# Hybrid pooling and state-space layer on one core: gate tiles reordered around the state-space projection, and branch merges cut into three steps

## The chip, the cores and the metric

The kernel runs on one core of a Trainium2 chip. The metric is device time in microseconds (us) of one launch. The engines are TensorE (PE, matrix products), VectorE (DVE), ScalarE (ACT), GpSimd (POOL, which here mostly issues transfers) and SyncE (SP, which issues the weight loads). Each engine takes its own instructions strictly in order and waits on semaphores for the others.

## What is computed

One layer of a hybrid encoder, in float32, for 256 prompt rows and 8 x 16 sample rows, so 384 rows (tokens) in all; model width 2048.

```python
proj  = rmsnorm(x) @ w_in                     # pool | z | xBC | dt | gates
gates = sigmoid(gate columns)                 # g_A and g_B, 2048 columns each
A     = pooled, mapped and scaled pool part   # 2048 wide
B     = gated_rmsnorm(ssd_scan(...), z)       # 4096 wide, norm over 8 groups of 512
m     = g_A * (A @ w_pool_proj) + g_B * (B @ w_ssd_proj)
x     = x + rmsnorm(m @ w_out)
x     = x + rmsnorm(relu(rmsnorm(x) @ w_up)**2 @ w_down)
```

The change lies around `B @ w_ssd_proj`, the product and sum that make `m`, and the start of `m @ w_out`.

## The kernel before, in words

**Products in float32.** Each float32 operand is split into a high part h and the rest l (fp32r). ACT makes h with a copy (L70 or L1120), DVE makes l with a subtraction (L71 or L1121). A product is three matmuls: h·h, l·h and h·l. Weights come in pieces of 128x1024 through SP.

**Gate tiles.** A gate tile is 128 of the 2048 gate columns for all 384 tokens. `proj` (L136) makes one in two halves; a half takes one weight piece and issues 24 matmuls (L101 to L103, 128x384). After each half a hook may run, which writes other work into the program at that point. `gate_b(i)` makes tile i of branch B: DVE scales it (L587), ACT takes the sigmoid (L588), POOL stores it in scratch memory `gb_scr` (L589). `gate_late(i)` makes tile i of branch A: scaling (L1311), sigmoid (L1312), then DVE multiplies it by the branch's pooled product, `ppt`, which POOL loads from `pp_scr` (L1309, L1313), and POOL stores the result in `ma_scr` (L1314). Gate work is issued on DVE and ACT behind the latest weight split (`later`).

**The last norm of branch B.** Before the stage begins, DVE normalises the last group of B (L191 to L193) and scales its four tiles (L925); POOL stores them in `a_scr` (L928). The projection reads B back from `a_scr` through SP (L1229, `ax`).

**The mixed stage.** `B @ w_ssd_proj` runs as 16 pairs ("quads") of seven forms each, 112 in all, which is Strassen's scheme with seven products for a two by two block. The weights of a form are b11, b21, U, b22, W, V or X; the activations are matching sums and differences. DVE makes the differences (L1235), ACT and DVE split them (L1242, L1243). U starts as the piece b12 in a buffer w_b, onto which POOL adds a second piece by an accumulating load (L1133). The forms are woven in between gate halves so that PE has both: the twelve tiles ga4 to ga15 (24 halves) and gb8 to gb12 (10 halves) call `hook`, 34 times in all. The first call takes the differences and four of the splits of quad 0, the second the other four, and from the third on `112 * (done - 2) // 32` forms have been issued. So three gate halves (ga4 and the first of ga5) stand on PE in front of the first form. Sums collect in `acc` (`acs`, `sq` in PSUM); at the end DVE turns each half of `acc` into four product blocks by seven additions (`converted`).

**The merges.** `merge(n)` makes tile n of m. POOL loads gate tile `gb` and the gated product `ma` (L1295, L1296), PE transposes three blocks of `acc` (L1299, tile `mt`), DVE multiplies (L1300) and adds (L1301), ACT and DVE split the result into mh and ml (L1302, L1303). Merges 0 to 3 lie inside the last quad, the tiles of the others, `gbr` and `mar`, have two buffers each.

**The last part.** Gate tiles gb13 to gb15 (six halves, no hook) follow, then the product with w_out: `moving` issues 18 matmuls (L154 to L156, 128x512) for a unit of 256 rows of w_out. Merges 4 and 5 stand ahead of unit 0, and merges 6+2i and 7+2i behind unit i, up to unit 4. The stage's memory is freed there, and units 5 to 7 come with the rest of w_out. Behind the layer's first half follow the up-projection (`pj_up`) and the down-projection, whose quads (`wd`) have the same seven forms and an accumulating load each.

Of the kernel before, what the change touches and what calls it, by code (L numbers as in the profile page):

```python
# [14 lines left out]
P = 128  # L15
T = 384
# [17 lines left out]
def build(ctx, tc, io):  # L34
    nc = tc.nc
    v, s, te, gp, sy = nc.vector, nc.scalar, nc.tensor, nc.gpsimd, nc.sync
# [179 lines left out]
    pp_scr = [dram.tile([P, T], F32, name=f"pp_scr{i}") for i in range(4, KD)]  # L216
# [871 lines left out]
    ms_ = []  # L1088
# [158 lines left out]
    def sp_quad(gk, np_):  # L1247
        def part(slot, k2):
            h, l = slots[gk][slot]
            return h[:, k2], l[:, k2]  # L1250

        def extra(i):
            t = np_ * 7 + i
            if gk and t < 3:
                refill(gk, ("W", "V", "X")[t])
            if gk == 7:
                if t in (7, 8):
                    for _ in range(4):
                        if todo:
                            todo.pop(0)()  # L1260
                elif 9 <= t < 13:
                    merge(t - 9)
                elif t == 13:
                    todo.extend(converted(lambda m: acc[:, 9 + m]))
                    while todo:
                        todo.pop(0)()
                elif t == 6:
                    todo.extend(converted(lambda m: acc[:, m]))
                elif t == 4:
                    spare.append(pq.tile([P, 10, 2, P], F32, tag="ax", name="axe").rearrange("p s k t -> p (s k t)"))  # L1270
# [12 lines left out]

    todo, spare = [], []

    def merge(n):
        if n < NE:
            gb, ma = (spare[0][:, i * T : i * T + T] for i in (n % 3 * 2, n % 3 * 2 + 1))
            h, l = early_tiles(("mh", "ml", ms_))
        else:  # L1290
            ma, gb = (mp.tile([P, T], F32, tag=f"{a}r", name=f"{a}r{n}", bufs=2) for a in ("ma", "gb"))
            h = mp.tile([P, T], F32R, name=f"mh{n}")
            l = mp.tile([P, T], F32R, name=f"ml{n}")
            ms_.append((h, l))
        gp.dma_start(gb, gb_scr[n])  # L1295
        gp.dma_start(ma, ma_scr[n])  # L1296
        o = sstile(f"mt{n}")[:, :T]
        for b in range(3):
            te.transpose(o[:, b * P : b * P + P], hacc(acc, b, n // 4)[:, n % 4 * P : n % 4 * P + P], ident)  # L1299
        v.tensor_tensor(gb, o, gb, ALU.mult)  # L1300
        v.tensor_tensor(ma, ma, gb, ALU.add)  # L1301
        s.activation(h, ma, AF.Copy)  # L1302
        v.tensor_tensor(l, ma, h.bitcast(F32), ALU.subtract)  # L1303

    def gate_late(i, hook):
        ps = proj([io["w_ga"][i, q] for q in range(2)], xg, f"ga{i}", hook)
        t = pq.tile([P, T], F32, tag="gt", name=f"gat{i}", bufs=2)
        pp = pq.tile([P, T], F32, tag="pt", name=f"ppt{i}")
        gp.dma_start(pp, pp_scr[i - 4])  # L1309
        with later():  # L1310
            v.tensor_tensor(halves(t), even_odd(ps), halves(rstd), ALU.mult)  # L1311
            s.activation(t, t, AF.Sigmoid)  # L1312
            v.tensor_tensor(t, t, pp, ALU.mult)  # L1313
        gp.dma_start(ma_scr[i], t)  # L1314

    aload(0)
    for gk in range(8):
# [3 lines left out]

    def hook():
        done_[0] += 1
        if done_[0] == 1:
            diffs(0)
            for key in ("b11", "s2", "b21", "U"):
                refill(0, key)
        elif done_[0] == 2:
            for key in ("b22", "W", "V", "X"):
                refill(0, key)  # L1330
        want = max(0, 112 * (done_[0] - 2) // (NH_ - 2))
        forms(want - done_[1])
        done_[1] = want

    for i in range(4, KD):
        gate_late(i, hook)
    for i in range(8, 13):
        gate_b(i, pq, "gt", hook, 2)
    assert not line
# [11 lines left out]
    def merges(*ns):  # L1351
        def go():
            for n in ns:
                merge(n)

        return go
# [39 lines left out]
    with tc.tile_pool(name="phf", bufs=1, side="right", reuse_waits="tile") as pf, tc.tile_pool(  # L1396
# [80 lines left out]
        for nb in range(4):  # L1477
            gpo = pf2.tile([P, 512], F32, tag="gpo", name=f"gpo{nb}", bufs=1)
            sy.dma_start(gpo, io["g_mix_post"][blk(nb)].partition_broadcast(P))
            s.activation(gpo, gpo, AF.Copy, scale=-0.5)  # L1480
            o = [sstile(f"wo{nb}_{b}") for b in range(3)] if nb else o_first

            def scaled(b, nb, o, gpo):
                return v.tensor_tensor(hm[:, b, blk(nb)], o[b], gpo, ALU.mult)

            def done(b):
                q = pf2.tile([P, 512], F32, tag="q", name=f"q1_{nb}_{b}", bufs=1)
                sq = lambda: s.activation(q, o[b], AF.Square, accum_out=st[:, b, nb : nb + 1])
# [18 lines left out]
            moving(  # L1507
                o,
                wo_units(nb),
                ms_,  # L1510
                5 if nb == 3 else 0,
                done,
                pk,
                5 if nb == 3 else 0,
                None,
                {(2, 3): first_turns} if nb == 3 else None,
                lo=0 if nb else 5,
            )
        phk.close()
        pga = upool.enter_context(tc.tile_pool(name="pga", bufs=1, reuse_waits="tile"))  # L1520
# [370 lines left out]
```

## Time and profile before

| | us |
|---|---|
| median of 3 runs | 2616.23 (2615.16 to 2618.46) |
| the profiled execution | 2614.65 |
| its span | 2612.7 |
| PE busy | 2580.1 |
| DVE busy | 1955.3 |
| ACT busy | 1597.7 |
| POOL busy | 425.4 |

The profile is of one execution. A span runs from the first to the last instruction; the profiled execution took 1.95 us more than its span. In a row of the timeline the columns are start, duration, engine, line, operation, what is written and what is read, and in brackets how long the engine had been idle and which instruction of which engine ended that. Rows with x2 or more are runs of equal instructions. A row of waits gives the sum, the count and the longest. A row of windows gives the stretch, its length and each engine's busy time (PE, PE's weight loads, DVE, ACT, POOL, with the number of instructions), then the clock that was granted to PE, the DMA engines' busy share and GB/s.

### The profile page before, as it was taken

To read this page: it belongs to the slowest core of one execution; us is meant where nothing else is said; L and a number is where in the kernel's file an instruction comes from. 1 tells how busy PE (TensorE), PEld (TensorE's weight loads), DVE (VectorE), ACT (ScalarE), POOL (GpSimd) and SP (SyncE) were. 2 spreads that over 40 slices of the span, in tenths; PEclk is the share of its full clock that TensorE was granted. 3 is DMA by queue.
4 is the path that set the end of the run, shared out by engine and by line. 5 is a ranking of instruction groups with operands and counts; after the bars stand their busy time and mean duration, and the time that the engine had idled before them with its cause. 6 is when DMAs were issued, how large, how long until landed. Compare 5 with 4: busy or idle time off the path is not lost.

```text
span 2612.7 us, 41084 instructions
## 1 busy us (share of the span) xinstructions
PE 2580.1 (99%) x15589; PEld 2452.8 (94%) x15589; DVE 1955.3 (75%) x2763; ACT 1597.7 (61%) x2520; POOL 425.4 (16%) x622
## 2 busy tenths in 40 slices
PE   9999999999999999899999989999999999999998
PEld 9999999999999999889999978999999999999997
DVE  6675367999999998588888755767777777777766
ACT  6443365657565756378888534666667676766653
POOL 0000043445444543110001010000000000000000
PEclk9999999999999999999999999999999999999999
DMA  7445466666666766576766365555545555555434
GB/s 277 150 137 163 158 223 212 238 214 234 228 238 209 237 228 226 198 220 196 209 192 204 132 214 172 198 161 167 154 151 157 167 171 154 154 153 163 143 133 174
DMA packets 151189, 490.42 MB, mean 188 GB/s; under 512 B 21728, under 2 KB 36896, under 8 KB 145232
## 3 DMA queue, kind: packets, MB, share of 16 engines
q1 hardware_dynamic: 111312, 358.29, 41.1%
q0 software_dynamic: 32624, 114.70, 15.4%
q10 hardware_dynamic: 7056, 14.81, 1.8%
q8 instruction: 122, 2.00, 0.3%
q14 instruction: 75, 0.61, 0.1%
HBM read 437.85 MB, written 49.87 MB: 187 GB/s over the span
## 4 chain that ended last, share of the span: by engine, by line
PE 95%; issue 2%; DVE 1%; DMA 1%; POOL 1%; ACT 0%; DVEq 0%; POOLq 0%; ACTq 0%
PE pj_up L101 6%; PE pj_up L103 6%; PE pj_up L102 6%; PE wd L1170 5%; PE wd L1169 5%; PE wd L1171 5%; PE pj_x L101 5%; PE pj_x L102 5%; PE pj_x L103 5%; PE pj_z L103 3%; PE pj_z L102 3%; PE pj_z L101 3%; PE sq L1170 3%; PE sq L1171 3%; PE sq L1169 3%
## 5 line engine op out<-in xcount | busy, mean ns | idle before, releaser
L101 PE MATMUL pj_up<-x1h,wh_up 128*128 128x384 f32 (+1 forms) x1024 | 333.7, 326 | 0.0
L102 PE MATMUL pj_up<-x1l,wh_up 128*128 128x384 f32 (+1 forms) x1024 | 333.4, 326 | 0.0
L103 PE MATMUL pj_up<-x1h,wl_up 128*128 128x384 f32 (+1 forms) x1024 | 333.4, 326 | 0.0
L70 ACT ACTIVATE wh_up<-w_up 128x1024 fp32r<-128x1024 f32 x126 | 133.2, 1057 | 219.6 <-PE pj_up L102 202.5
L101 PE MATMUL pj_x<-xgh,wh_x 128*128 128x384 f32 x768 | 251.9, 328 | 0.0
L102 PE MATMUL pj_x<-xgl,wh_x 128*128 128x384 f32 x768 | 250.4, 326 | 0.0
L103 PE MATMUL pj_x<-xgh,wl_x 128*128 128x384 f32 x768 | 250.4, 326 | 0.0
L71 DVE TENSOR_TENSOR wl_up<-w_up,wh_up 128x1024 fp32r<-128x1024 f32 x126 | 154.1, 1223 | 57.7 <-ACT wh_up L70 57.2
L102 PEld LDWEIGHTS pj_up<-x1l,wh_up 128*128 128x128 f32 x1024 | 193.6, 189 | 2.6
L101 PEld LDWEIGHTS pj_up<-x1h,wh_up 128*128 128x128 f32 x1024 | 193.6, 189 | 2.6
L103 PEld LDWEIGHTS pj_up<-x1h,wl_up 128*128 128x128 f32 x1024 | 193.6, 189 | 0.0
L101 PE MATMUL pj_z<-xgh,wh_z 128*128 128x384 f32 x512 | 166.9, 326 | 0.0
L102 PE MATMUL pj_z<-xgl,wh_z 128*128 128x384 f32 x512 | 166.9, 326 | 0.0
L103 PE MATMUL pj_z<-xgh,wl_z 128*128 128x384 f32 x512 | 166.9, 326 | 0.0
L1133 POOL DMA_DIRECT2D w_b_wd<-w_down x28 | 24.2, 865 | 773.2 <-DMA w_b_wd<-w_down 742.5
L101 PEld LDWEIGHTS pj_x<-xgh,wh_x 128*128 128x128 f32 x768 | 145.1, 189 | 2.1 <-issue 0.4
L102 PEld LDWEIGHTS pj_x<-xgl,wh_x 128*128 128x128 f32 x768 | 145.2, 189 | 0.0
L103 PEld LDWEIGHTS pj_x<-xgh,wl_x 128*128 128x128 f32 x768 | 145.2, 189 | 0.0
L71 DVE TENSOR_TENSOR wl_x<-w_x,wh_x 128x1024 fp32r<-128x1024 f32 x96 | 116.8, 1221 | 30.1 <-ACT wh_x L70 30.1
L70 ACT ACTIVATE wh_x<-w_x 128x1024 fp32r<-128x1024 f32 x96 | 100.3, 1052 | 59.9 <-PE pj_z L102 30.9
L1146 ACT COPY acc<-wd 128x512 f32<-128x512 f32 x200 | 116.5, 583 | 23.0 <-PE wd L1171 22.9
L1169 PE MATMUL wd<-wh_b_wd,fh 128*128 128x512 f32 x336 | 127.3, 379 | 0.0
(478 smaller groups left out, 7827.8 us busy)
## 6 DMA issues: line engine op xcount, KB each, us to landing
w_up<-w_up SPq DMA_DIRECT2D x128, 512.0 KB, 4.1
w_b_wd<-w_down SPq DMA_DIRECT2D x112, 512.0 KB, 4.5
w_x<-w_in SPq DMA_DIRECT2D x96, 512.0 KB, 4.0
w_z<-w_in SPq DMA_DIRECT2D x64, 512.0 KB, 4.0
w_b_sq<-w_ssd SPq DMA_DIRECT2D x64, 512.0 KB, 4.3
w_ga<-w_ga SPq DMA_DIRECT2D x32, 512.0 KB, 3.9
w_pp<-w_pp SPq DMA_DIRECT2D x32, 512.0 KB, 3.5
hs<-ssm POOLq DMA_DIRECT2D x16, 1024.0 KB, 7.2
```

The lines of the kernel that those rows point to most:

```text
L70: cut[0] = s.activation(h, w, AF.Copy)
L71: cut[1] = v.tensor_tensor(l, w, h.bitcast(F32), ALU.subtract)
L101: te.matmul(out, wh, xh, start=first, stop=False, **how)
L102: te.matmul(out, wh, xl, start=False, stop=False, **how)
L103: return te.matmul(out, wl, xh, start=False, stop=last, **how)
L1133: gp.dma_start(w, unit(0, np_ * 2), accum_op=ALU.add)
L1146: s.copy(dst, o)
L1169: te.matmul(out, mh, vh, start=begin, stop=False, skip_group_check=held)
L1170: te.matmul(out, mh, vl, start=False, stop=False, skip_group_check=held)
L1171: te.matmul(out, ml, vh, start=False, stop=end, skip_group_check=held)
```

## The change

Three things are moved.

- **First end.** gb8 and gb9 now come ahead of ga4, so four plain gate halves stand in front of the forms. Hooks 2 and 3 hold the differences and splits of quad 0, and the 112 forms are spread over 31 hooks in place of 32. In `gate_late` the product with `ppt` and the store in `ma_scr` are kept back (`late`) and issued at the first hook of the next gate tile, and the load of `ppt` is issued at the first hook of its own tile.
- **Merges.** `merge` becomes `fetch` (two loads), `gated` (transposes, multiply, add) and `parts` (the split). The tiles of merges 0 to 2 lie in the free `ax` buffer; the others, `mw`, in the seven buffers "wd" that held the quads' weights. A pair of loads now needs a buffer that was freed by the merge seven places before, in place of two.
- **Second end.** Inside the last quad DVE makes one addition of the first conversion for each form from t = 7 on, and no merge. The second conversion and merges 0 to 9 are put at the hooks of gb13 to gb15 (`turns`). During w_out block 0 the three steps of a merge stand behind different units; six units (not five) run before the stage's memory is freed.

```diff
@@ sp_quad.extra, last quad
-                if t in (7, 8):
-                    for _ in range(4):
-                        if todo:
-                            todo.pop(0)()
-                elif 9 <= t < 13:
-                    merge(t - 9)
-                elif t == 13:
-                    todo.extend(converted(lambda m: acc[:, 9 + m]))
-                    while todo:
-                        todo.pop(0)()
+                if t == 4:
+                    early = pq.tile([P, 10, 2, P], F32, tag="ax", name="axe").rearrange("p s k t -> p (s k t)")
+                    for n in range(3):
+                        place[n] = early[:, n * 768 : n * 768 + 768]
+                        fetch(n)
                 elif t == 6:
                     todo.extend(converted(lambda m: acc[:, m]))
+                elif t > 6:
+                    todo.pop(0)()
@@ gate_late
+        def both():
+            if not pp:
+                while late:
+                    late.pop(0)()
+                pp.append(pq.tile([P, T], F32, tag="pt", name=f"ppt{i}"))
+                gp.dma_start(pp[0], pp_scr[i - 4])
+            hook()
...
-            v.tensor_tensor(t, t, pp, ALU.mult)
-        gp.dma_start(ma_scr[i], t)
+        def product():
+            v.tensor_tensor(t, t, pp[0], ALU.mult)
+            gp.dma_start(ma_scr[i], t)
+        late.append(product)
@@ hook and the gate tiles
-        want = max(0, 112 * (done_[0] - 2) // (NH_ - 2))
+        want = max(0, 112 * (done_[0] - 3) // (NH_ - 3))
...
+    for i in range(8, 10):
+        gate_b(i, pq, "gt", hook, 2)
     for i in range(4, KD):
         gate_late(i, hook)
-    for i in range(8, 13):
-        gate_b(i, pq, "gt", hook, 2)
+    for i in range(10, 13):
+        gate_b(i, pq, "gt", hooked, 2)
...
+    turns = [
+        do((gated, (0, 1)), (parts, (0, 1))),
+        do((gated, (2,)), (parts, (2,)), (fetch, (6, 7))),
+        do((gated, (3, 4)), (parts, (3,))),
+        do((close_half, (0,)), (gated, (5, 6))),
+        do((fetch, range(8, 11)), (gated, (7, 8))),
+        do((gated, (9,))),
+    ]
+    do((fetch, (3, 4, 5)))()
     for i in range(13, KD):
-        gate_b(i, pq, "gt", None, 2)
+        gate_b(i, pq, "gt", lambda: turns.pop(0)(), 2)
...
-    merge(4)
-    merge(5)
-    moving(o_first, wo_units(0), ms_, 0, None, None, 0, {i: merges(6 + 2 * i, 7 + 2 * i) for i in range(5)}, lo=0, hi=5)
+    do((parts, (4, 5)), (fetch, (11, 12)))()
+    between_ = {
+        0: do((parts, (6, 7)), (fetch, (13, 14)), (gated, (10,))),
+        1: do((parts, (8, 9)), (fetch, (15,)), (gated, (11,))),
+        2: do((parts, (10, 11)), (gated, (12,))),
+        3: do((parts, (12,)), (gated, (13,))),
+        4: do((parts, (13,)), (gated, (14, 15))),
+        5: do((parts, (14, 15))),
+    }
+    moving(o_first, wo_units(0), ms_, 0, None, None, 0, between_, lo=0, hi=6)
```

How the change moves instructions is seen in three places. The first is DVE at the first end, from the last of the four products on the last group of B. Before (`gat` is gate tile ga4, `alb` and `als` the low parts of the activations, `ax` the differences of quad 0):

```order
L925 SCALAR_TENSOR_TENSOR zs_3_11577<-zs_3_11577,vec,ny_g_12299 128x384
L1311 TENSOR_TENSOR gat_12436<-pj_ga_12338,rstd 128x384
L1313 TENSOR_TENSOR gat_12436<-gat_12436,ppt_12437 128x384
L1243 TENSOR_TENSOR alb_12375<-ax_12333,ahb_12374 128x256
L1243 TENSOR_TENSOR als_12379<-ax_12333,ahs_12378 128x256
L1235 TENSOR_TENSOR ax_12333<-ax_12333 128x256 x5
```

The same place now, with `gbt` for the gate tiles gb8 and gb9:

```order
L925 SCALAR_TENSOR_TENSOR zs_3_11577<-zs_3_11577,vec,ny_g_12299 128x384
L587 TENSOR_TENSOR gbt_12420<-pj_gb_12338,rstd 128x384
L1243 TENSOR_TENSOR alb_12405<-ax_12333,ahb_12404 128x256
L1243 TENSOR_TENSOR als_12409<-ax_12333,ahs_12408 128x256
L587 TENSOR_TENSOR gbt_12563<-pj_gb_12424,rstd 128x384
L1235 TENSOR_TENSOR ax_12333<-ax_12333 128x256 x5
```

The product that reads `ppt` no longer stands ahead of the differences; the scaling of gb9 stands there, which reads the PSUM tile of the fourth gate half and writes a tile whose memory held the last of the four products (`zs_3`), so that it also waits until POOL's store of that tile has landed.

The second place is POOL's queue in the mixed stage, at the accumulating load of the fifth quad (`w_b_sq_0`). Before:

```order
L1314 DMA ma_scr_123<-gat_13069 128x384
L1309 DMA ppt_13294<-pp_scr_108 128x384
L1133 DMA w_b_sq_0_13331<-w_ssd 128x1024
L1314 DMA ma_scr_124<-gat_13293 128x384
L1309 DMA ppt_13510<-pp_scr_109 128x384
```

And now:

```order
L1327 DMA ma_scr_121<-gat_13012 128x384
L1316 DMA ppt_13048<-pp_scr_106 128x384
L1133 DMA w_b_sq_0_13357<-w_ssd 128x1024
L1327 DMA ma_scr_122<-gat_13229 128x384
L1316 DMA ppt_13265<-pp_scr_107 128x384
```

The load stands behind the gated product of ga5 (121) where it stood behind that of ga7 (123).

The third place is POOL's queue at the second end, from the store of gate tile gb13 (`gb_scr_145`) on. Before, from there to the fourth pair of loads:

```order
L589 DMA gb_scr_145<-gbt_16028 128x384
L589 DMA gb_scr_146<-gbt_16093 128x384
L1295 DMA gbr_16171<-gb_scr_136 128x384
L1296 DMA mar_16170<-ma_scr_120 128x384
L589 DMA gb_scr_147<-gbt_16158 128x384
L1295 DMA gbr_16185<-gb_scr_137 128x384
L1296 DMA mar_16184<-ma_scr_121 128x384
L1295 DMA gbr_16223<-gb_scr_138 128x384
L1296 DMA mar_16222<-ma_scr_122 128x384
```

And now, from the same store:

```order
L589 DMA gb_scr_145<-gbt_16024 128x384
L1284 DMA mw_16165<-gb_scr_142 128x384
L1285 DMA mw_16165<-ma_scr_126 128x384
L589 DMA gb_scr_146<-gbt_16124 128x384
L589 DMA gb_scr_147<-gbt_16216 128x384
L1284 DMA mw_16236<-gb_scr_143 128x384
L1285 DMA mw_16236<-ma_scr_127 128x384
L1284 DMA mw_16239<-gb_scr_144 128x384
L1285 DMA mw_16239<-ma_scr_128 128x384
```

At the store of gb14 the loads stood at merge 4 (`gb_scr_136`) and now stand past merge 10 (`gb_scr_142`); the last loads, of merges 13 to 15 (`gb_scr_145` to 147), still follow the stores of the gate tiles that they read.

More of the change, by code (lines that the diff above doesn't have):

```diff
@@ L1282, in sp_quad, with fetch, gated @@
         return quad(f"sq{gk}_{np_}", pq, acc, np_, gk == 0, lambda i, nb: io["w_ssd"][nb, gk * 2 + i], part, extra)
[L1284 to L1296, printed above, removed]
+    todo, place = [], {}
+    def fetch(n):
+        if n not in place:
+            place[n] = pq.tile([P, 1024], F32, tag="wd", name=f"mw{n}", bufs=7)
+        gp.dma_start(place[n][:, :T], gb_scr[n])
+        gp.dma_start(place[n][:, T : 2 * T], ma_scr[n])
+    def gated(n):
+        gb, ma = place[n][:, :T], place[n][:, T : 2 * T]
         o = sstile(f"mt{n}")[:, :T]
@@ L1301, in merge, with parts @@
         v.tensor_tensor(ma, ma, gb, ALU.add)
+    def parts(n):
+        ma = place[n][:, T : 2 * T]
+        if n < NE:
+            h, l = early_tiles(("mh", "ml", ms_))
+        else:
+            h = mp.tile([P, T], F32R, name=f"mh{n}")
+            l = mp.tile([P, T], F32R, name=f"ml{n}")
+            ms_.append((h, l))
         s.activation(h, ma, AF.Copy)
         v.tensor_tensor(l, ma, h.bitcast(F32), ALU.subtract)
+    late = []
     def gate_late(i, hook):
-        ps = proj([io["w_ga"][i, q] for q in range(2)], xg, f"ga{i}", hook)
+        pp = []
+        def both():
[5 more added lines that the diff above has]
+            hook()
+        ps = proj([io["w_ga"][i, q] for q in range(2)], xg, f"ga{i}", both)
         t = pq.tile([P, T], F32, tag="gt", name=f"gat{i}", bufs=2)
-        pp = pq.tile([P, T], F32, tag="pt", name=f"ppt{i}")
-        gp.dma_start(pp, pp_scr[i - 4])
         with later():
@@ L1323, in hook @@
         done_[0] += 1
-        if done_[0] == 1:
+        if done_[0] == 2:
             diffs(0)
@@ L1327, in hook, with hooked, do, go @@
                 refill(0, key)
-        elif done_[0] == 2:
+        elif done_[0] == 3:
             for key in ("b22", "W", "V", "X"):
                 refill(0, key)
-        want = max(0, 112 * (done_[0] - 2) // (NH_ - 2))
+        want = max(0, 112 * (done_[0] - 3) // (NH_ - 3))
         forms(want - done_[1])
         done_[1] = want
+    def hooked():
+        while late:
+            late.pop(0)()
+        hook()
+    for i in range(8, 10):
+        gate_b(i, pq, "gt", hook, 2)
     for i in range(4, KD):
         gate_late(i, hook)
-    for i in range(8, 13):
-        gate_b(i, pq, "gt", hook, 2)
-    assert not line
+    for i in range(10, 13):
+        gate_b(i, pq, "gt", hooked, 2)
+    assert not line and not todo
+    def do(*fns):
+        def go():
+            for fn, ns in fns:
+                for n in ns:
+                    fn(n)
+        return go
+    def close_half(_):
+        for fn in converted(lambda m: acc[:, 9 + m]):
+            fn()
     queue.extend((io["w_gb"][i, q], f"gb{i}_{q}") for i in range(13, KD) for q in range(2))
     queue.extend((io["w_out"][nb, kp], f"wo{nb}_{kp}") for nb in range(4) for kp in range(8 if nb < 3 else 3))
+    turns = [
[7 more added lines that the diff above has]
+    do((fetch, (3, 4, 5)))()
     for i in range(13, KD):
-        gate_b(i, pq, "gt", None, 2)
+        gate_b(i, pq, "gt", lambda: turns.pop(0)(), 2)
     main.close()
@@ L1347, in build @@
     o_first = [sstile(f"wo0_{b}") for b in range(3)]
-    merge(4)
-    merge(5)
[L1351 to L1356, printed above, removed]
-    moving(o_first, wo_units(0), ms_, 0, None, None, 0, {i: merges(6 + 2 * i, 7 + 2 * i) for i in range(5)}, lo=0, hi=5)
+    do((parts, (4, 5)), (fetch, (11, 12)))()
[8 more added lines that the diff above has]
+    moving(o_first, wo_units(0), ms_, 0, None, None, 0, between_, lo=0, hi=6)
     phe.close()
@@ L1516, in build @@
                 {(2, 3): first_turns} if nb == 3 else None,
-                lo=0 if nb else 5,
+                lo=0 if nb else 6,
             )
```

2 lines of the change are left out of this document (removed).

## The prediction

> **What bounds the kernel now.** I read the page first, then the waits of PE over the whole run, then windows around the places where PE waits, then the timeline there.
>
> ```profile
> span 2612.7 us, 41084 instructions
> PE 2580.1 (99%) x15589; PEld 2452.8 (94%) x15589; DVE 1955.3 (75%) x2763; ACT 1597.7 (61%) x2520; POOL 425.4 (16%) x622
> ```
>
> PE is busy for all but 32.6 us of the span. The change leaves PE's matmuls as they are, so it can only win where PE waits or runs slowly. The waits of PE, largest first (sum, count, longest):
>
> ```profile
> PE sq L1169 <- ACT wh_b_sq L1120: 11.3, 1, 11.3
> PE mt L1299 <- DVE gbr L1300: 4.4, 5, 1.6
> PE wo L154 <- ACT mh L1302: 3.8, 1, 3.8
> PE pj_gb L103 <- DVE wl_gb L71: 1.4, 1, 1.4
> PE sq L1170 <- DVE wl_b_sq L1121: 0.9, 1, 0.9
> PE pj_gb L101 <- ACT wh_gb L70: 0.7, 1, 0.7
> PE wo L156 <- DVE ml L1303: 0.2, 1, 0.2
> ```
>
> Two places hold nearly all of it: 12.2 us at the first form (L1169, L1170), and 4.4 + 3.8 + 1.4 + 0.7 + 0.2 = 10.5 us around the merges. Windows at the first end and in the mixed stage (length, PE busy, PE's loads, DVE, ACT, POOL, clock, DMA share, GB/s):
>
> ```profile
> 1105.00:1120.00 15.00, 5.10 (x12) 3.69 (x13) 9.21 (x19) 5.82 (x10) 1.99 (x3) 0.54 0.71 198
> 1200.00:1420.00 220.00, 220.00 (x1138) 201.85 (x1137) 186.44 (x222) 179.16 (x280) 17.24 (x26) 1.00 0.68 201
> ```
>
> Between the ends PE is never idle, DVE is busy 186.44 / 220 = 85% and ACT 81%: there the stage is PE's.
>
> **First end: one more gate half in front of the first form.** The chain that ends last today:
>
> ```profile
> 1099.51 2.14 POOL L928 DMA_DIRECT2D a_scr<-zs  x4 [6.56 <-DVE zs L925]
> 1102.41 0.33 PE L103 MATMUL pj_ga<-xgh,wl_ga 128*128 128x384 f32 x1
> 1109.48 0.56 DVE L1313 TENSOR_TENSOR gat<-gat,ppt 128x384 f32<-128x384 f32 x1 [8.21 <-DMA ppt<-pp_scr]
> 1109.95 0.42 DVE L1243 TENSOR_TENSOR alb<-ax,ahb 128x256 fp32r<-128x256 f32 x1
> 1110.62 1.76 DVE L1235 TENSOR_TENSOR ax<-ax 128x256 f32<-128x256 f32 x5
> 1114.05 0.80 PE L1169 MATMUL sq<-wh_b_sq,ahb 128*128 128x512 f32 x1 [11.31 <-ACT wh_b_sq L1120]
> 1116.12 0.80 PE L1170 MATMUL sq<-wl_b_sq,ahb 128*128 128x512 f32 x1 [0.85 <-DVE wl_b_sq L1121]
> ```
>
> DVE stands still for 8.21 us on the `ppt` load, which is queued on POOL behind the four stores of `a_scr`. The differences (L1235) stand behind it, so ACT and PE wait too. The release at 1109.48 comes 1116.12 - 1109.48 = 6.64 us before PE runs freely.
>
> The change takes the product out of that place, but puts the scaling of gb9 there. This waits for the landing of the last `a_scr` store. How late is that? The transfers of this place (KB each, median us to landing):
>
> ```profile
> a_scr<-zs POOLq DMA_DIRECT2D x2, 192.0 KB, 7.6
> ppt<-pp_scr POOLq DMA_DIRECT2D x1, 192.0 KB, 7.7
> ```
>
> The stores are issued from 1099.51 to 1101.65, a quarter of 2.14 us each, the last at 1101.1; with 7.6 us it lands at 1108.7. `ppt`, issued at 1101.65, took 7.8; with that the store lands at 1108.9. The norm's chain on DVE also takes in one weight split of the added half. A split's duration is seen further on:
>
> ```profile
> 1531.75 1.23 DVE L71 TENSOR_TENSOR wl_wo<-w_wo,wh_wo 128x1024 fp32r<-128x1024 f32 x1 [0.39 <-ACT wh_wo L70]
> ```
>
> So the stores start 1.2 us later and the last one lands at 1109.9 to 1110.1. Behind it the scaling replaces the product at an equal price, and the low parts (1110.62 - 1109.95 = 0.67 us) now run ahead of the wait. PE is free at 1110.1 + 6.64 - 0.67 = 1116.1, as now (1116.12). But by then it has done one gate half more. Its price is 24 matmuls, by these rows:
>
> ```profile
> 1472.21 0.33 PE L101 MATMUL pj_gb<-xgh,wh_gb 128*128 128x384 f32 x1
> 1473.99 0.33 PE L103 MATMUL pj_gb<-xgh,wl_gb 128*128 128x384 f32 x1
> ```
>
> Eleven steps in 1.78 us are 0.162 each, so 3.9 us a half. **First term: 3.8 us won**, a tenth under the half, since gb9's sigmoid also stands ahead of some splits on ACT; a wait of some 7.5 us is left. The bounds: SP now issues the quad's weight pieces later, so that more of them may fall on the stores; if a store then takes the 9.1 us that loads of w_b_wd take (row further on), 1.4 us less, 2.4. If the store lands before PE ends gb9 (1102.7 + 3.9 = 1106.6), only PE's own half binds, 3.5 us earlier: 7 us. A remaining wait of 7.5 us should leave the slow restart as it is: the clock was 0.54 in that window.
>
> The Trainium skill (DMA: Bandwidth & Descriptors, section Queues, rings and completion order) says that each DMA engine goes round between the queues it has work for. By an equal share the stores would land sooner than they did, which is the case of rival 2 below. The trace speaks against it with 7.6 us for 192 KB.
>
> **The mixed stage.** The 112 forms now share 31 hooks, 3.6 a half instead of 3.5. PE's order changes, not its work; DVE's 85% rises by less than a point: cost nothing, hidden under PE's 220 of 220 us, and bounded by the 15% that DVE has free. The later product also holds back its `ma_scr` store on POOL and with it the accumulating load behind:
>
> ```profile
> 1176.68 0.95 POOL L1133 DMA_DIRECT2D w_b_sq<-w_ssd  x1
> 1205.75 1.06 ACT L1120 ACTIVATE wh_U_sq<-w_b_sq 128x1024 fp32r<-128x1024 f32 x1 [0.73 <-PE pj_ga L102]
> w_b_sq<-w_ssd POOLq DMA_DIRECT2D x4, 512.0 KB, 8.4
> ```
>
> U's split comes 1205.75 - 1176.68 - 8.4 = 20.7 us after the landing and waits for PE, not for the load. A gate half with its forms takes (1468.07 - 1114.05) / 32 = 11 us (the first from a row below), so the delay fits. Cost nothing.
>
> **Second end.** From the first matmul of gb13 to the eleventh unit of w_out:
>
> ```profile
> 1468.07 0.33 PE L101 MATMUL pj_gb<-xgh,wh_gb 128*128 128x384 f32 x1
> 1498.68 0.82 PE L1299 MATMUL mt<-cst,acs 128*128 128x128 f32 x6
> 1499.25 0.46 PE L154 MATMUL wo<-wh_wo,mh 128*128 128x512 f32 x1
> 1535.81 0.56 DVE L1300 TENSOR_TENSOR gbr<-mt,gbr 128x384 f32<-128x384 f32 x1 [1.43 <-DMA gbr<-gb_scr]
> 1537.45 0.79 PE L154 MATMUL wo<-wh_wo,mh 128*128 128x512 f32 x1 [3.82 <-ACT mh L1302]
> 1538.03 0.63 PE L155 MATMUL wo<-wl_wo,mh 128*128 128x512 f32 x1
> 1542.30 0.62 PE L154 MATMUL wo<-wh_wo,mh 128*128 128x512 f32 x1
> 1550.09 0.38 PE L154 MATMUL wo<-wh_wo,mh 128*128 128x512 f32 x1
> 1552.03 0.38 PE L154 MATMUL wo<-wh_wo,mh 128*128 128x512 f32 x1
> ```
>
> That is 1552.03 - 1468.07 = 83.96 us. The work in it: 6 halves of 3.9 = 23.4; 10 units of 18 matmuls at 1.94 / 9 = 0.2155, 38.8; 12 merges' transposes at 0.57 / 2, 3.4; together 65.6. So 18.3 us are lost: 10.5 in the waits; 2.1 in matmuls at half speed behind the longest of them (from 1538.03 to 1542.30 ten steps take 4.27 us instead of 2.16); 5.7 in what these rows don't show, other slow steps and hand-overs between transposes and matmuls. The cause is in the DVE row: the multiplication waits for its load, since a pair of loads may only start when an earlier merge has freed one of two buffers.
>
> With seven buffers and loads ahead, the loads of merges 0 to 10 are issued before the first unit, and each of the others has two units or more (2 x 18 x 0.2155 = 7.8 us) between the freeing merge and its use. The transfers took 3.1 and 3.8 us there:
>
> ```profile
> gbr<-gb_scr POOLq DMA_DIRECT2D x12, 192.0 KB, 3.1
> mar<-ma_scr POOLq DMA_DIRECT2D x12, 192.0 KB, 3.8
> ```
>
> What is late next is DVE. In the six halves it now has six splits (1.23), 27 instructions of 384 columns (two for each of ten merges, four low parts, three scalings; 0.47 each, as from the row of 1109.48 to the next) and seven additions of 512 columns, by the columns about 0.63 each: 7.4 + 12.7 + 4.4 = 24.5 us, beside 23.4 + 10 x 0.285 = 26.2 us of PE. It fits with 6% to spare; the half with the seven additions is covered by splits made up to three pieces ahead. **Second term:** the waits, the slow steps and two thirds of the rest go: 10.5 + 2.1 + 3.9 = 16.5 us. Bounds: 10.5 (waits alone) and 18.3. Merges 0 to 3 only move; their transposes cost PE the same elsewhere.
>
> The Trainium skill (TensorE: Matmul & The Clock Gate, Part 1) says that PE falls to half clock after an idle window of about 3.4 us and needs as much sustained work to come back. The trace agrees: half clock follows the 3.82 us wait. By that rule the slow steps go with the waits, and at the first end a rest of 7.5 us keeps the slow restart.
>
> **Further on.** SP now issues all four pieces of the first down-projection quad behind further pieces of w_up, at about the time of the first row here, where today those of the next quad stand:
>
> ```profile
> 1666.04 0.93 SPq L1130 DMA_DIRECT2D w_b_wd<-w_down  x2
> 1675.10 1.06 ACT L1120 ACTIVATE wh_b_wd<-w_b_wd 128x1024 fp32r<-128x1024 f32 x1 [0.19 <-PE pj_up L102]
> w_b_wd<-w_down SPq DMA_DIRECT2D x6, 512.0 KB, 9.1
> ```
>
> The second of them, needed at 1675.10, lands near 1666.5 + 9.1 = 1675.6. **Third term: 0.5 us lost**, bounds 0 and 3.
>
> **The sum.** 3.8 + 16.5 - 0.5 = 19.8 us. The profiled execution goes from 2614.65 to 2594.85; it lies 1.58 us below the median, so the median goes from 2616.23 to 2596.4.
>
> **The rivals.**
> 1. *The first end pays nothing.* The landing of `a_scr` takes the place of `ppt` and slips by another 3.8 us, as SP's weight pieces now fall on it. For it: the DMA engines are 71% busy there. Against it: pieces load beside the stores today too. 2596.4 + 3.8 = 2600.2.
> 2. *The first end pays in full.* The stores land before PE has done gb9, and only DVE's and ACT's chain behind it is left: 7 us, 2593.2. Against it: that takes a landing within 4.3 us (1106.6 less 1102.3).
> 3. *The second end pays half.* DVE, with 6% to spare, makes PE wait at some splits, or the last loads come late beside weights. Then 8 of the 16.5: 2604.9.
> 4. *Slower.* In the mixed stage each accumulating load stands on POOL behind a store that waits for the delayed product. Were U late, PE would wait at each of 13 quads. This decides from 1.5 us a quad on (13 x 1.5 = 19.5); at 3 us late the time would be 2596.4 + 39 = 2635. The 20.7 us of slack speak against it, and the load now stands behind the product of two tiles earlier.
> 5. *It does nothing.* The waits at both ends only move to other queues: 2614 to 2618. No row supports it.
>
> **How the numbers follow.** Forecast 0.51, rival 1 0.13, rival 2 0.06, rival 3 0.22, rival 4 0.03, rival 5 0.05. By the terms' own bounds, 7 + 18.3 gives 2590.9 and 2.4 + 10.5 - 3 gives 2606.3. The range 2591 to 2606 holds rivals 1 to 3 as well and leaves out 4 and 5 and the worst of 3. A measurement of this kernel can tell about 0.2% (5.2 us) from no change. The forecast and rivals 1 to 3 lie beyond it: faster 0.92, same 0.05, slower 0.03.
>
> **What would show it.** In the changed profile the wait of PE at the first form should be 7 to 8 us and end on the same ACT row, with DVE's wait before it ended by the `a_scr` store. No PE wait longer than 1 us should stand between 1440 and 1550, the clock should be full there, and the stretch from gb13 to the eleventh unit should take some 68.6 us (84.0 - 16.5, and 4 x 0.285 for the transposes of merges 0 to 3 that move into it). Behind the first quad no row of ACT may wait for an accumulating load. The prediction is wrong if PE waits for wl_gb or wl_wo at the second end for several us, or if the first wait stays above 11.

## The result and the profile after

The changed kernel takes 2600.72 us (median of 4 runs, 2599.84 to 2604.61) beside 2616.40 us before (4 runs): 15.7 us less, a ratio of 0.9942 with a 95% interval of 0.9925 to 0.9959. The forecast was 2596.4 us, 19.8 us less; the measured time lies in its range of 2591 to 2606. The profiled execution took 2600.41 us with this span and these busy times:

```profile
span 2598.4 us, 41070 instructions
PE 2575.4 (99%) x15589; PEld 2447.4 (94%) x15589; DVE 1952.1 (75%) x2763; ACT 1597.8 (61%) x2520; POOL 424.0 (16%) x622
```

PE's waits over the whole run (sum, count, longest) have changed in kind; left out are a wait of 1.2 us for `warm` at the kernel's start, the same in both kernels, and three waits of 0.2 to 0.4 us:

```profile
PE sq L1169 <- ACT wh_b_sq L1120: 6.8, 1, 6.8
PE sq L1170 <- DVE wl_b_sq L1121: 2.4, 4, 0.9
PE wo L155 <- DVE wl_wo L71: 1.0, 2, 0.8
PE pj_p L101 <- ACT wh_e L309: 1.0, 1, 1.0
PE sq L1170 <- DVE wl_W_sq L1121: 0.5, 1, 0.5
PE sq L1170 <- DVE wl_V_sq L1121: 0.4, 1, 0.4
```

The waits around the merges (`mt`, `mh`) are gone, and the first form waits 6.8 us instead of 11.3. New are waits for the low parts of forms in the middle of the mixed stage (three of the four on wl_b, and those on wl_W and wl_V) and for those of w_out.

**Where the time went, by stage.** The same instructions of PE mark the same places in both traces. Before:

```profile
1090.71 0.33 PE L208 MATMUL bc_g<-nl_g,onesr 128*128 128x384 f32 x1
1122.63 0.38 PE L1169 MATMUL sq<-wh_U_sq,ahU 128*128 128x512 f32 x1
1551.39 0.38 PE L154 MATMUL wo<-wh_wo,mh 128*128 128x512 f32 x1
1637.52 0.38 PE L156 MATMUL wo<-eh_wo,ml 128*128 128x512 f32 x1
```

After, with the first matmul of gb13, which stood at 1468.07 before:

```profile
1090.34 0.33 PE L208 MATMUL bc_g<-nl_g,onesr 128*128 128x384 f32 x1
1122.64 0.38 PE L1169 MATMUL sq<-wh_U_sq,ahU 128*128 128x512 f32 x1
1467.60 0.33 PE L101 MATMUL pj_gb<-xgh,wh_gb 128*128 128x384 f32 x1
1535.60 0.38 PE L154 MATMUL wo<-wh_wo,mh 128*128 128x512 f32 x1
1623.19 0.38 PE L156 MATMUL wo<-eh_wo,ml 128*128 128x512 f32 x1
```

These are the last matmul of the norm's broadcast, the first of the U form of quad 0, the first of gb13, the first of the eleventh unit of w_out and the last of w_out. (The prediction put the eleventh unit at 1552.03; by the count of matmuls it begins at 1551.39.) The differences, after less before:

| stage | before, us | after, us | difference |
|---|---|---|---|
| start to the norm's broadcast | 1090.71 | 1090.34 | -0.37 |
| broadcast to the U form of quad 0 (one gate half more now) | 31.92 | 32.30 | +0.38 |
| U form to gb13 (one gate half and four merges' transposes less now) | 345.44 | 344.96 | -0.48 |
| gb13 to the eleventh unit (four merges' transposes more now) | 83.32 | 68.00 | -15.32 |
| eleventh unit to the end of w_out | 86.13 | 87.59 | +1.46 |
| sum | | | -14.33 |

The spans differ by 14.3 us, so nothing is left for what follows. The first end has won 3.9 - 0.38 = 3.5 us. But the mixed stage is only 0.48 us shorter, though 3.9 us of gate half and 1.0 us of transposes have left it: it lost 4.4 us. And the rest of w_out lost 1.5 us.

### The profile page after: what moved, and what is told of

It is laid out like the page before. It is cut to its first block, busy times and chain, and to the rows that moved or that the text cites. A ratio compares the mean times of both kernels' runs of the same rounds, so it can differ in the third digit from the quotient of the medians.

```text
span 2598.4 us, 41070 instructions
## 1 busy us (share of the span) xinstructions
PE 2575.4 (99%) x15589; PEld 2447.4 (94%) x15589; DVE 1952.1 (75%) x2763; ACT 1597.8 (61%) x2520; POOL 424.0 (16%) x622
## 3 DMA queue, kind: packets, MB, share of 16 engines
q0 software_dynamic: 32624, 114.70, 15.3%
## 4 chain that ended last, share of the span: by engine, by line
PE 93%; DMA 2%; issue 2%; DVE 2%; ACT 1%; POOL 0%; SPq 0%; DVEq 0%; POOLq 0%; ACTq 0%
PE pj_up L101 6%; PE pj_up L102 6%; PE pj_up L103 6%; PE wd L1171 5%; PE wd L1170 5%; PE wd L1169 5%; PE pj_x L101 5%; PE pj_x L102 5%; PE pj_x L103 5%; PE pj_z L101 3%; PE pj_z L103 3%; PE pj_z L102 3%; PE sq L1170 2%; PE sq L1171 2%; PE sq L1169 2%
```

## The experiments

All times of stages below are between the marks of the table: "front" is the broadcast to the U form, "mixed" the U form to gb13, "end" gb13 to the eleventh unit, "rest" the eleventh unit to the end of w_out. A single time stands where there was one run; a run is beside before on the same chip (medians there 2617.31, 2616.66 and 2616.17 us).

| kernel | time, us | front | mixed | end | rest |
|---|---|---|---|---|---|
| before | 2616.40 | 31.92 | 345.44 | 83.32 | 86.13 |
| after | 2600.72 | 32.30 | 344.96 | 68.00 | 87.59 |
| e1 first end alone | 2621.63 | 31.64 | 346.74 | 88.30 | 86.13 |
| e2 second end alone | 2598.98 | 31.96 | 344.10 | 68.43 | 87.61 |
| e3 after, ax held back | 2595.47 | 32.32 | 340.28 | 67.52 | 87.02 |
| e4 after, even spread | 2595.93 | 32.41 | 339.74 | 68.71 | 87.02 |
| e5 e4, other tile for gb9 | 2595.84 | 30.19 | 341.32 | 68.48 | 87.61 |
| e6 e4, x later | 2592.38 | 32.89 | 339.92 | 67.52 | 86.13 |
| e7 e4, merges in one piece | 2595.60 | 31.04 | 341.98 | 68.54 | 87.35 |
| e8 e7, two buffers | 2602.57 | 31.50 | 340.50 | 73.78 | 88.77 |
| e9 before, x later | 2614.14 | 33.46 | 345.43 | 82.05 | 86.13 |
| e10 e4, product early | 2595.03 | 31.57 | 340.44 | 68.52 | 86.43 |
| e11 e4 + edits of e5, e6 | 2592.47 | 28.45 | 342.79 | 67.52 | 86.13 |
| e12 e1, even spread | 2615.60 | 31.69 | 341.06 | 88.61 | 86.13 |

How far a stage of one execution can be read is seen in e4, e6, e7 and e8, which have the same program up to gb13: their fronts take 31.04 to 32.89 us, their mixed stages 339.74 to 341.98, and the two together 371.99 to 373.02. So about 2 us in front or mixed alone, and about 1 us in their sum, can be the spread between executions.

**What the mixed stage lost.** Three places lose it: near 1212, 1301 and 1394 us PE's waits and lengthened steps cost about 1.6, 1.1 and 2.3 us. The first, in the changed kernel:

```profile
1203.41 2.52 SPq L1229 DMA_DIRECT2D ax<-a_scr  x4
1208.41 1.22 DVE L1156 TENSOR_TENSOR w_b_sq<-w_b_sq,w_b_sq 128x1024 f32<-128x1024 f32 x1
1209.63 0.42 ACT L1242 ACTIVATE ahs<-ax 128x256 fp32r<-128x256 f32 x1 [2.45 <-DMA ax<-a_scr]
1210.87 0.42 DVE L1235 TENSOR_TENSOR ax<-ax 128x256 f32<-128x256 f32 x1 [1.24 <-DMA ax<-a_scr]
1212.56 1.23 DVE L1121 TENSOR_TENSOR wl_b_sq<-w_b_sq,wh_b_sq 128x1024 fp32r<-128x1024 f32 x1
1213.84 0.48 PE L1170 MATMUL sq<-wl_b_sq,ahb 128*128 128x512 f32 x1 [0.78 <-DVE wl_b_sq L1121]
```

ACT and DVE have reached an instruction that reads `ax`, the activations of the next quad, which nobody needs yet. It has been loading since 1203.4 and has not landed. Both engines stand, and the weight split of the current quad (wl_b) stands behind. Over the whole mixed stage ACT and DVE wait for these loads in the changed kernel like this, and before not at all:

```profile
ACT ahs L1242 <- DMA ax<-a_scr: 8.7, 5, 3.1
DVE ax L1235 <- DMA ax<-a_scr: 3.5, 2, 2.3
```

The order of DVE shows the move: before, the first difference of the next quad's `ax` stood behind the split of the W form in six of the seven quads that make it; now it stands two splits earlier, behind that of U, in two of those six, and these are the first and the third of the three places. At the second, ACT alone stands on `ax` (3.06 us), and DVE waits for ACT. That gave theory A. The rivals were B (DVE has too much to do wherever four forms fall between two gate halves, whatever stands there) and C (the delayed product is in the way).

**e1 and e2: each end alone.** e1 is the kernel before with the hunks of the change on `gate_late`, `hook` and the gate tiles; e2 is the changed kernel with those three as before.

> The first end of the change alone (gb8 and gb9 first, 31 hooks, late product), the merges as before. Theory A (in the changed kernel the mixed stage, from the U form of the first quad to gb13, loses 5.3 us instead of 0.9 because the next quad's activations ax stand on ACT and DVE ahead of the landing of their loads) and theory B (DVE is over-full wherever four forms fall between two gate halves) and theory C (the late product) all expect: first end 3.5 us won, mixed stage about 4.4 us lost, so 0.9 us above before, 2617. The rival that the loss comes from the second end's new queue orders: mixed stage loses 0.9 as before, 2612.9.

> The second end of the change alone (merges in three steps, loads ahead), the first end as before. A, B and C: from gb13 to the eleventh unit of w_out 68.0 us instead of 83.3, the mixed stage loses about 0.9 us less the transposes moved out, the rest of w_out loses 1.5 us more as in the changed kernel: 13.9 us below before, 2602.5. If the loss in the mixed stage belongs to this end: 2607.

e1 took 2621.63 us (10 runs), a ratio of 1.0019 to before (1.0009 to 1.0028): 0.2% slower, where 2617 was expected. The first end is won as in the full change, and the mixed stage loses 1.3 + 3.9 = 5.2 us in comparison; not expected was that the old second end now takes 88.30 us, 5.0 us longer. e2 took 2598.98 us, a ratio of 0.9934 (0.9919 to 0.9948), 3.5 us less than expected: its end takes 68.43 us, and its mixed stage loses nothing, where 0.9 us was expected. So the loss of the mixed stage belongs to the first end's part of the change, and the second end alone gives as much as the whole change.

**e3: ax held back.** The changed kernel, in which the differences and splits of the next quad are issued on ACT and DVE behind the W split of the quad's first half; `behind` orders an instruction behind another on its engine.

```diff
+        if name.startswith("W_sq") and name.endswith("_0"):
+            pin[:] = [a, d]
...
-                diffs(gk + 1)
+                with pinned():
+                    diffs(gk + 1)
```

(`refill(gk + 1, ...)` likewise; `pinned` puts its block behind `pin[0]` on ACT and `pin[1]` on DVE.)

> The changed kernel with the differences and splits of the next quad's activations held back on DVE and ACT until behind the W split of the quad's first half. Theory A: the waits of ACT and DVE for ax go and the mixed stage's loss falls from 5.3 to about 1 us: 4.3 us below the changed kernel, 2596.4. Theory B: the loss stays at 5 us, 2600.7. Theory C: it stays too.

2595.47 us, a ratio of 0.9918 (0.9903 to 0.9933). Its mixed stage takes 340.28 us, 4.7 us less than in the changed kernel with the same spread and the same late product; ACT and DVE no longer wait for `ax`. Between 1200 and 1420 us PE is busy 220.00 of 220 us in e3 and 217.50 in the changed kernel (first e3, then the changed kernel):

```profile
1200.00:1420.00 220.00, 220.00 (x1136) 201.75 (x1135) 187.33 (x225) 180.76 (x280) 19.85 (x29) 1.00 0.68 200
```

```profile
1200.00:1420.00 220.00, 217.50 (x1110) 196.61 (x1110) 183.70 (x221) 175.46 (x272) 17.56 (x27) 1.00 0.67 196
```

DVE is busier in e3 (187.33) than in the changed kernel (183.70), and PE waits less. A holds; B and C, by which the loss would have stayed, fall.

**e4: an even spread.** The changed kernel with 3.5 forms a hook as before, and one more at each of the last four.

```diff
-        want = max(0, 112 * (done_[0] - 3) // (NH_ - 3))
+        h = max(0, done_[0] - 3)
+        want = 7 * h // 2 + max(0, h - 27)
```

> The changed kernel with 3.5 forms at each hook as before, and the four left over one each at the last four hooks. Theory A: DVE's order around ax is that of before again, loss about 1 us, 4.3 us below the changed kernel, 2596.4. Theory B: the loss goes except in the last four halves, 1 to 2.5 us left, 2597 to 2598. Theory C: the loss stays at 5 us, 2600.7.

2595.93 us, 0.9919 (0.9902 to 0.9935); mixed 339.74 us. DVE's order around `ax` is that of before again, and 0.4 us of waiting for it is left. So what moved `ax` forward was the change from 3.5 to 3.6 forms a hook: with it the gate halves drift through the quads, and the instructions on `ax` come up at other moments.

**e5: what the first form waits for.** e4 with gb9's tile in the buffer of `ppt`, whose memory did not hold the last group of B.

```diff
-    for i in range(8, 10):
-        gate_b(i, pq, "gt", hook, 2)
+    gate_b(8, pq, "gt", hook, 2)
+    gate_b(9, pq, "pt", hook)
```

> The even spread of e4 with the tile of gb9 in the buffer of ppt, whose memory did not hold the last group of B. If the first form waits for the landing of the a_scr stores only through that tile, DVE scales gb9 as soon as PE has made it, and the first form starts 1.5 to 2.5 us earlier (then the quad's weight pieces are last): from the end of the norm's broadcast to the first U form 30 to 31 us instead of 32.4. Rival: the weight pieces or the activations are as late as the stores, 32 to 32.4 us.

PE's wait at the first form falls from 7.1 us in e4 to 5.2, and the front takes 30.19 us, 2.2 less. But the mixed stage takes 1.6 us more, and the time hardly moves (2595.84 us). Three rows of e5 in order of time:

```profile
1107.09 0.56 DVE L587 TENSOR_TENSOR gbt<-pj_gb,rstd 128x384 f32<-128x384 f32 x1 [1.26 <-PE pj_gb L103]
1118.38 1.06 ACT L1120 ACTIVATE wh_U_sq<-w_b_sq 128x1024 fp32r<-128x1024 f32 x1 [4.93 <-DMA w_b_sq<-w_ssd]
1124.40 0.43 PE L103 MATMUL pj_ga<-xgh,wl_ga 128*128 128x384 f32 x1 [1.31 <-DVE wl_ga L71]
```

DVE scales gb9 as soon as PE has made it. Then U of quad 0, the accumulating load, is the next thing late: ACT waits 4.93 us for it, and the gate split behind it on DVE makes PE wait 1.31 us. This is not new in e5: ACT waits 3.60 us for the same load in e4, and in e7, whose front is that of e4, ACT waits 4.45 us and PE 1.97. So the shorter wait at the first form is shown (e11 has 5.3 us too; all other kernels with gb8 and gb9 first have 6.3 to 7.3); that it is U which takes the gain back is the likely reading, and the size, 1.6 us, is within the spread.

**e6: x later.** In the changed kernel the rest of w_out had a new wait. PE's row there, last, and the ACT rows that it goes back to:

```profile
1528.94 0.63 ACT L1523 ACTIVATE gpo<-gpo 128x512 f32<-128x512 f32 x1 [8.06 <-DMA gpo<-g_mix_post]
1538.17 0.63 ACT L1523 ACTIVATE gpo<-gpo 128x512 f32<-128x512 f32 x1 [4.70 <-DMA gpo<-g_mix_post]
1541.06 0.48 PE L155 MATMUL wo<-wl_wo,mh 128*128 128x512 f32 x1 [0.78 <-DVE wl_wo L71]
```

ACT stands on the loads of the gain `gpo`, and weight splits are queued behind. The first load is late and delays what uses it; the gain has one buffer, so the second load is issued only at 1533.60, behind the last use of the first, and the weight splits behind the second ACT row are those that PE waits for. (Behind the first ACT row PE waits only 0.22 us, still in the end stage.) The three loads of x (1 MB each) were issued on POOL at 1514.7, some 5 us ahead of gpo; before, they came at 1525.9 and 1532.2, behind gpo. e6 puts them behind gpo:

```diff
-    for b in range(3):
-        gp.dma_start(x1[:, b, :], io["x_tok"][b])
...
-            sy.dma_start(gpo, io["g_mix_post"][blk(nb)].partition_broadcast(P))
+            with behind(sy.dma_start(gpo, io["g_mix_post"][blk(nb)].partition_broadcast(P))):
+                if nb < 3:
+                    sy.dma_start(x1[:, nb, :], io["x_tok"][nb])
```

> The even spread of e4 with the three loads of x (1 MB each) issued one by one behind the loads of the gain gpo on SP instead of all at once on POOL ahead of them. If the new loss of 0.9 to 1.5 us in the rest of w_out comes from ACT waiting for gpo, which lands late beside x, ACT's wait for gpo falls from 8.8 to under 4 us and the rest of w_out takes 86.1 us as before. Rival (DVE's own order): 87.0.

The first wait for gpo falls to 3.91 us. The second is 6.03 us, longer than before the edit, but it ends early enough that PE does not wait. The rest of w_out takes 86.13 us, as before:

```profile
1519.05 0.63 ACT L1524 ACTIVATE gpo<-gpo 128x512 f32<-128x512 f32 x1 [3.91 <-DMA gpo<-g_mix_post]
```

The end is 1.2 us shorter than in e4 as well (67.52 us): the steps of PE that are late behind the first gpo row cost e4 1.2 us there, the changed kernel 0.5 and e3 nothing, so this part varies from execution to execution. The time is 2592.38 us.

**e7 and e8: what carried the second end.** e7 is e4 with each merge in one piece (`gated` and `parts` together) and in the places of before; the loads stay ahead, in seven buffers. e8 is e7 with two buffers from merge 3 on.

```diff
+    def both(n):
+        gated(n)
+        parts(n)
...
+    between_ = {
+        0: do((both, (6, 7)), (fetch, (13, 14))),
+        1: do((both, (8, 9)), (fetch, (15,))),
+        2: do((both, (10, 11))),
+        3: do((both, (12, 13))),
+        4: do((both, (14, 15))),
+    }
@@ e8, in both(n), in place of the other fetches
+        if 3 <= n < 14:
+            place[n + 2] = place[n]
+            fetch(n + 2)
```

> The even spread of e4 with each merge in one piece again and in the places of before (4 and 5 ahead of unit 0, 6 + 2i and 7 + 2i behind unit i), the loads ahead in seven buffers. Theory L (the loads ahead carry the gain of the second end): gb13 to the eleventh unit takes 68.7 to 71 us. Rival S (cutting the merges carries it): 76 us or more.

> As e7, and a pair of loads from merge 5 on waits again for the merge two places earlier (two buffers). Theory L: the waits of before come back, gb13 to the eleventh unit takes 79 to 85 us. Rival S: no more than 3 us over e7.

e7's end takes 68.54 us, e4's 68.71: that the merges are cut is worth nothing that can be seen. e8's end takes 73.78 us, and the wait of before is back:

```profile
PE mt L1291 <- DVE mw L1292: 4.9, 3, 1.7
```

So seven buffers are worth 5.2 us in this stretch; 79 to 85 was wrong, and so was the rival's limit of 3 us. The larger part, from 83.32 to 73.78 (and 1.1 us more, since four merges' transposes now lie in this stretch), remains with two buffers. PE's waits say which part that is: e8 has the waits for the merges' multiplications (4.9 us; 4.4 before), but no longer the waits at the first halves of gb13 (1.4 and 0.7 us before) and for the last merge's mh (3.8 us before, with slow steps behind it).

**e9: x later, in the kernel before.** The edit of e6 in the kernel before.

> The kernel before with only the loads of x moved: one by one behind gpo on SP, not on POOL among the last merges' loads. If these 3 MB are what made the last merges late (the wait of 3.8 us for mh and the half clock behind it), gb13 to the eleventh unit takes 76 to 79 us instead of 83.3. If not, 82 us or more; then the rest of the second end's gain lies in DVE's work moved out of the last quad.

82.05 us, so the "if not" holds: the loads of x account for 1.3 us at most of this one execution's stretch, which is no more than stages vary by. The wait for mh is 2.1 us instead of 3.8:

```profile
PE wo L154 <- ACT mh L1302: 2.1, 1, 2.1
```

By exclusion the larger part of the second end's gain, about 10 us, goes with what e8 keeps of the change: the additions of the conversions and merges 0 to 3 no longer fall on DVE together in the last quad, and merges 4 and 5 are loaded ahead of the stores of gb14 and gb15, not behind them. These two were not tried apart, so which of them takes away the wait at gb13 and which the wait for mh is not shown.

**e10: the gated product back in its own tile.** e4 with `gate_late` as before.

> The even spread of e4 with the gated product back in its own gate tile. The product is off the way in every theory that is left: front to gb13 372.1 us as in e4, within 0.7 us, and the second end 68.7. If the late product is needed (theory C turned round): 373.5 us or more.

31.57 + 340.44 = 372.01 us from the broadcast to gb13, against 372.15 in e4; 2595.03 us. So with the even spread the late product is worth nothing that can be seen, and costs nothing.

**e12: the first end alone, with the even spread.**

> The first end alone as in e1, but with the even spread. If e1's losses in the mixed stage (1.3 us more in spite of 3.9 us less work) and in the second end (5.0 us more) both come from the shifted spread: mixed stage 341 us, second end 83.3 us, in all 4 us below before. If only the mixed stage's: second end 88 us, 1 us above before.

The mixed stage is whole again: front and mixed take 372.75 us, 4.6 less than before. But the old second end takes 88.61 us, 5.3 more. PE's waits in e12's end:

```profile
PE mt L1299 <- DVE gbr L1300: 4.0, 4, 1.3
PE wo L154 <- ACT mh L1302: 3.9, 1, 3.9
PE pj_gb L103 <- DVE wl_gb L71: 3.7, 1, 3.7
PE pj_gb L101 <- ACT wh_gb L70: 1.3, 1, 1.3
```

PE's wait for wl_gb at the first half of gb13 was 1.4 us before and is 3.7 here: DVE comes out of the last quad later than before. What makes it later was not tried by itself; e12 issues one form more than the even 3.5 at each of its last four hooks, and e1 3.6 on average at every hook. So the first end alone is worth nothing with the old second end, most likely because DVE's work for that end stands in the last quad.

**e11: together.** e4 with the edits of e5 and e6.

> Even spread, the other tile for gb9 and the later loads of x together. The stages add: front and mixed stage 371.5 us, second end 67.5 to 68.7, rest of w_out 86.1: 1.0 to 1.5 us below e4's stages, 2594.5 us as a median, and 22 us below before. If the transfers of x collide with something else: as e4, 2596.

2592.47 us (2592.10 to 2594.93, 4 runs), a ratio to before of 0.9915 (0.9898 to 0.9932). Front and mixed take 371.24 us, end 67.52, rest 86.13: 524.89 us in all, against 532.85 in the changed kernel and 546.81 before. So it is 8.0 us ahead of the changed kernel by the stages; the intervals of the two ratios still overlap a little. e3 (527.14) and e4 (527.88) can be told from it by the stages only. The one run of e6 was as fast (2592.38 us), so the edit of e5 adds nothing that shows in the time: its gain is given back in the mixed stage here too (342.79), and 28.45 us in front is partly a quick return of PE to full speed (see the last section).

## Why the prediction was right in sign and 4 us too good

- **First term, 3.8 us: right, and as close as 3.5 us partly by luck.** The mechanism is the one forecast: DVE's scaling of gb9 waits for the landing of the `a_scr` store. PE's wait is 6.8 us (7 to 8 forecast), 4.5 us less than before. But from the first form's start to U's PE took 9.55 us, 1.0 more than before (8.59), since its slow steps lasted longer, and this varies without any change of the program: 7.96 to 9.90 us in e4, e6, e7 and e8.

```profile
1105.93 0.33 PE L103 MATMUL pj_gb<-xgh,wl_gb 128*128 128x384 f32 x1
1109.20 0.56 DVE L587 TENSOR_TENSOR gbt<-pj_gb,rstd 128x384 f32<-128x384 f32 x1 [4.41 <-DMA a_scr<-zs]
1113.09 0.80 PE L1169 MATMUL sq<-wh_b_sq,ahb 128*128 128x512 f32 x1 [6.83 <-ACT wh_b_sq L1120]
1115.16 0.80 PE L1170 MATMUL sq<-wl_b_sq,ahb 128*128 128x512 f32 x1 [0.85 <-DVE wl_b_sq L1121]
```

The store landed at 1109.2 where 1109.9 to 1110.1 was worked out, and DVE's wait ended there. Rival 2's 7 us did not come, and e5 suggests that its next wait was wrong: with the store out of the way the first form still waits 5.2 us, and the accumulating load of U is late behind it.

- **The mixed stage, "cost nothing, hidden under PE's 220 of 220 us, and bounded by the 15% that DVE has free": this step failed.** It cost 4.4 us. The step counted DVE's work, which did not rise, and followed one queue, POOL's accumulating load, which was not late. It did not ask where the other instructions of the stage would stand once the gate halves drifted: two engines that work in order met a load that had not landed. e3 and e4 show it, and that DVE's free share was not what decided it.

- **Second term, 16.5 us: right in sum.** The stretch fell by 15.3 us, with 4 x 0.285 = 1.1 us of transposes moved into it: 16.5. It takes 68.0 us where 68.6 was forecast, and PE is busy 67.78 us of it at full clock. Before and after:

```profile
1468.07:1551.39 83.32, 72.80 (x362) 63.66 (x361) 47.82 (x69) 27.78 (x42) 16.10 (x30) 0.94 0.64 216
```

```profile
1467.60:1535.60 68.00, 67.78 (x373) 62.24 (x372) 48.60 (x76) 27.72 (x42) 9.58 (x18) 1.00 0.66 224
```

Its cause was only half right: "a pair of loads may only start when an earlier merge has freed one of two buffers" carries 5.2 us (e8), not all; the waits at gb13 and for the last merge's mh went by other parts of the change, which were not tried apart. DVE's work in this stretch, named as what would be late next, fitted.

- **A wait that no term held: gpo, 1.5 us lost.** The change issues x's loads earlier, since the merges' loads in front of them on POOL are done earlier; the prediction followed POOL's queue up to the last merge and not to x. e6 shows it.

- **Third term, 0.5 us lost: nothing.** The stretches behind w_out are equal.

- Rivals 1, 3, 4 and 5 did not come: both ends paid, U's loads were not late behind the delayed product, and e10 shows the product's place not to matter.

In sum: -3.5 + 4.4 - 16.5 + 1.5 = -14.1; with -0.4 ahead of all of this and 0.1 to 0.2 for the moved transposes it is the -14.3 of the spans, where -3.8 - 16.5 + 0.5 = -19.8 was forecast.

## What to carry to other kernels

Where several engines work in order, a change in how work is interleaved also moves instructions that the change doesn't name; look for those that wait for a load, and at what stands behind them, for they cost 4.4 us here though DVE was busy only 183.70 of 220 us. Hold back an instruction that is not needed yet until its data has surely landed. And where a queue is made faster, follow it to its end: the next transfers in it start earlier and, as x and gpo here, can fall on others.

## What the runs showed of the hardware

- PE's return to full speed after a wait takes long, and not equally long. After the wait of 6.83 us in the changed kernel the steps stay at 0.43 us, twice the 0.2155 of full speed, until 1120.45, 7.4 us after the first form's start at 1113.09, with a pause of 0.85 us in between:

```profile
1120.02 0.63 PE L1170 MATMUL sq<-wl_b_sq,ahb 128*128 128x512 f32 x1
1120.45 0.42 PE L1171 MATMUL sq<-wh_b_sq,alb 128*128 128x512 f32 x1
1120.70 0.38 PE L1169 MATMUL sq<-wh_b_sq,ahb 128*128 128x512 f32 x1
```

In e7, whose program is the same up to this place, they are over 4.7 us after the first form's start:

```profile
1112.66 0.79 PE L1169 MATMUL sq<-wh_b_sq,ahb 128*128 128x512 f32 x1 [7.15 <-ACT wh_b_sq L1120]
1117.02 0.52 PE L1171 MATMUL sq<-wh_b_sq,als 128*128 128x512 f32 x1
1117.38 0.38 PE L1169 MATMUL sq<-wh_b_sq,ahs 128*128 128x512 f32 x1
```

Over all runs it took 3.5 us (e11, with almost no pause) to 8.2 us (e6). The Trainium skill (TensorE: Matmul & The Clock Gate, Part 1) gives at least one busy window of about 3.4 us for the way back; counted from the first form's start every run took longer than that, up to more than twice as long.

- A load of 256 KB (gpo) that was issued 4.6 us behind 3 MB of other loads landed 9.6 us after its issue and made ACT wait 8.06 us; in e6, with the first MB of x issued 0.4 us behind it, it landed after 5.5 us and ACT waited 3.91.
